# Ranked experts with places of 192, 128 and 64 rows, the outer two with transposed gate and up products

## The chip, the cores and the metric

One NeuronCore of a Trainium2 chip. The metric is the device time of one execution in microseconds (us). Engines: PE is TensorE's matmul side and PEld its loads of stationary operands, DVE is VectorE, ACT ScalarE, POOL GpSimd, SP SyncE, which issues most DMAs.

## What is computed

Two layers of a backbone on 256 context and 512 latent tokens of width 1024. Each layer mixes tokens and then runs a mixture of 16 experts, of which every token takes two. Layer 0 routes all 768 tokens (1536 pairs of token and expert), layer 1 the 512 latent ones (1024 pairs). The part that the change touches is this:

```python
def moe_ffn(h, w_router, b_router, w_e_gate, w_e_up, w_e_down):
    ...
    hid = jax.nn.silu(rows @ w_e_gate[e]) * (rows @ w_e_up[e])
    return hid @ w_e_down[e]
    ...
    return jnp.einsum("nk,nkd->nd", weight.astype(h.dtype), pair_out)
```

`rows` are the tokens of one expert. Gate and up are 1024 x 512, down is 512 x 1024, all float32. How many rows an expert has depends on the router and is known only while the kernel runs.

## The kernel before

`backbone` runs for each layer the mixers, `merge` (which ends with the router's logits), `route` and `moe`. The experts' stage is `moe`.

**Products in three parts.** A float32 operand is split into a high part (ScalarE rounds it to float32r) and a low part (VectorE subtracts, L2228), and a product is high x high + high x low + low x high, three matmuls each (`mm3`, L1323 to L1330). The first operand of a matmul is the stationary one, which TensorE loads (PEld), the second is streamed past it.

**Which expert runs where.** `route` counts the rows of the experts. Experts 15 and 14 run first, in that order. The others get ranks: those with over 128 rows first, then the rest by number (L2116 to L2126). The first `R.nd` ranks (4 in layer 0, 2 in layer 1) have places for two blocks of 128 rows, the other ranks one block. `ORDER` (L39) says in which order the ranks run. The expert of a rank is read from `R.exps` into a register of SyncE when its weights are to be loaded (L2303). What has no place is run behind the rest by `chain` (L2326), one block of 128 rows per pass, each with all six units of weights.

**One expert** (`run`, L2290). Six weight units of 1 MB each (two halves of gate, of up and of down) are loaded by SyncE's queue and split (`unit`, L2214). `front` (L2231) gathers a block of 128 rows by an indirect DMA of POOL, transposes it with eight matmuls against the identity (L2251) and splits it into `xh` and `xl`, 128 x 8 x 128 each. `front` of the next expert is issued ahead of this expert's `gate_up`. `gate_up` (L2257) has the rows as stationary operand and 512 columns of weights as the streamed one: 24 matmuls into one PSUM bank for gate, 24 for up. The activation makes the hidden rows, 128 x 512. `down` (L2273) transposes them with four matmuls (L2279), splits them (L2280, L2281), runs 2 x 12 matmuls of 512 columns, scales on ScalarE (L2286) and scatters with an indirect DMA of POOL (L2287).

PSUM has eight banks: one for the transposes of x, four for gate and up, one for the transposes of the hidden rows, two for down. `HILO` (5 and 6) is the number of buffers of split weight units. In layer 0 the tables of layer 1's S5 branch (`s5_build`) are worked out between the experts.

The order of instructions on each engine is set by the tile framework's scheduler from the program's order and its own estimate of times.

Of the kernel before, what the change touches and what calls it, by code (L numbers as in the profile page):

```python
# [7 lines left out]
F32 = mybir.dt.float32  # L8
F32R = mybir.dt.float32r
# [8 lines left out]
NT = 6  # L18

# [19 lines left out]
ORDER = ((4, 0, 5, 6, 1, 7, 8, 2, 9, 10, 3, 11, 12, 13), (2, 3, 4, 5, 0, 6, 7, 8, 1, 9, 10, 11, 12, 13))  # L39


def const_blob():
# [16 lines left out]
        tok=p[:, None] + 128 * np.arange(6)[None, :], exp=np.arange(16)[None, :] * 768 + 0 * k,  # L59
# [1926 lines left out]
def route(K, l, lg, R):  # L1986
# [12 lines left out]
    n = NT - T0  # L1999
# [116 lines left out]
    over = tl([128, 14], "over")  # L2116
    inc, pre_, a0 = (tl([128, 14], x) for x in ("inc", "pre_", "a0"))
    V.tensor_scalar(over, cnt[:, 0:14], 128.5, None, op0=OP.is_gt)
    V.tensor_tensor_scan(inc, K.c("one")[:, 0:14], over, 0.0, OP.mult, OP.add)
    V.tensor_sub(pre_, inc, over)  # L2120
    V.scalar_tensor_tensor(a0, num[:, 0:14], inc[:, 13:14], pre_, op0=OP.add, op1=OP.subtract)
    V.tensor_sub(pre_, pre_, a0)
    V.tensor_mul(pre_, pre_, over)
    ranks = tl([128, 15], "ranks")
    V.tensor_add(ranks[:, 0:14], a0, pre_)
    V.tensor_copy(ranks[:, 14:15], num[:, 14:15])  # L2126
    er = tl([1, 14, 14], "er")
    V.tensor_tensor(er, ranks[0:1, None, 0:14].to_broadcast([1, 14, 14]), num[0:1, 0:14, None].to_broadcast([1, 14, 14]), op=OP.is_equal)
# [6 lines left out]
    V.scalar_tensor_tensor(tm.rearrange("p k t e -> p (k t) e"), ranks[:, None].to_broadcast([128, 2 * n, 15]), 1.0,  # L2135
                           sel[:, :, :, 0:15].rearrange("p k t e -> p (k t) e"), op0=OP.add, op1=OP.mult)
# [22 lines left out]
    V.tensor_scalar(c, cnt[0:1], 127.0, None, op0=OP.add)  # L2159
# [3 lines left out]
    V.tensor_scalar(c, c, -1.0, 0.0, op0=OP.add, op1=OP.max)  # L2163
    dbl = tl([1, 16], "dbl")
    V.memset(dbl, 0.0)
    V.scalar_tensor_tensor(dbl[:, 0:14], ranks[0:1, 0:14], float(R.nd), over[0:1], op0=OP.is_lt, op1=OP.mult)
    V.tensor_sub(c, c, dbl)
# [10 lines left out]
    V.tensor_add(a_, a_, dbl[:, None, :].to_broadcast(shp))  # L2178
    V.scalar_tensor_tensor(a_, a_, 1.0, b_, op0=OP.add, op1=OP.mult)
    V.tensor_mul(b_, b_, num[0:1, None, :].to_broadcast(shp))  # L2180
    V.tensor_reduce(o_[:, 1:13], b_, axis=AX.X, op=OP.add)
    V.scalar_tensor_tensor(a_, b_, 6.0, a_, op0=OP.mult, op1=OP.add)
# [8 lines left out]
def moe(K, l, fd, metad, R, pd, ra, na, routing, rest, tds):  # L2191
# [39 lines left out]
    def front(c, src):  # L2231

        if c:
            tok, pair, wt = (a[:, src:src + 1] for a in (c.tok, c.pair, c.wt))
        else:
            mt = p.tile([128, 4], I32, tag="mt", bufs=4, name="mt")
            nc.sync.dma_start(mt, src)
            wt = p.tile([128, 1], F32, tag="wt", bufs=4, name="wt")
            nc.vector.tensor_scalar(wt, mt[:, 2:3].bitcast(F32), 0.5, None, op0=OP.mult)
            tok, pair = mt[:, 0:1], mt[:, 1:2]  # L2240
        x = p.tile([128, D], F32, tag="x", bufs=2, name="x")
        nc.gpsimd.memset(x, 0.0)
        gathers.append(nc.gpsimd.indirect_dma_start(out=x[:], out_offset=None, in_=fd,
                                                    in_offset=bass.IndirectOffsetOnAxis(ap=tok, axis=0),
                                                    bounds_check=ntok - 1, oob_is_err=False))
        xh = p.tile([128, 8, 128], F32R, tag="xh", bufs=3, name="xh")
        xl = p.tile([128, 8, 128], F32R, tag="xl", bufs=3, name="xl")
        for g in range(2):
            ps = pp.tile([128, 512], F32, tag="t", bufs=1, name="pt")
            for k in range(4):  # L2250
                nc.tensor.transpose(ps[:, k * 128:(k + 1) * 128], x[:, (4 * g + k) * 128:(4 * g + k + 1) * 128], K.c("id"))  # L2251
            h_, l_ = (a[:, 4 * g:4 * g + 4].rearrange(f) for a in (xh, xl))
            nc.scalar.activation(h_, ps, AF.Copy)
            nc.vector.tensor_sub(l_, ps, h_.bitcast(F32))
        return pair, wt, xh, xl

    def gate_up(frs, us):  # L2257
        gu = [[], []]
        for j in range(2):
            for i, (_, _, xh, xl) in enumerate(frs):  # L2260
                ps = pp.tile([128, 512], F32, tag="g", bufs=4, name="pg")
                mm3(nc, ps, [(xh[:, k], xl[:, k], us[2 * j + k // 4][0][:, k % 4], us[2 * j + k // 4][1][:, k % 4]) for k in range(8)])
                gu[i].append(ps)
        hds = []
        for i in range(len(frs)):
            hd = p.tile([128, 512], F32, tag="hd", bufs=2, name="hd")
            nc.scalar.activation(hd, gu[i][0], AF.Tanh, scale=0.5)
            nc.vector.scalar_tensor_tensor(hd, hd, 1.0, gu[i][0], op0=OP.add, op1=OP.mult)
            nc.vector.tensor_mul(hd, hd, gu[i][1])
            hds.append(hd)  # L2270
        return hds

    def down(fr, hd, us):  # L2273
        pair, wt, _, _ = fr
        hh = p.tile([128, 4, 128], F32R, tag="hh", bufs=2, name="hh")
        hl = p.tile([128, 4, 128], F32R, tag="hl", bufs=2, name="hl")
        ps = pp.tile([128, 512], F32, tag="h", bufs=1, name="ph")
        for k in range(4):
            nc.tensor.transpose(ps[:, k * 128:(k + 1) * 128], hd[:, k * 128:(k + 1) * 128], K.c("id"))  # L2279
        nc.scalar.activation(hh.rearrange(f), ps, AF.Copy)  # L2280
        nc.vector.tensor_sub(hl.rearrange(f), ps, hh.rearrange(f).bitcast(F32))  # L2281
        o = p.tile([128, D], F32, tag="o", bufs=2, name="o")
        for n in range(2):
            ps = pp.tile([128, 512], F32, tag="d", bufs=2, name="pd")
            mm3(nc, ps, [(hh[:, k], hl[:, k], us[n][0][:, k], us[n][1][:, k]) for k in range(4)])
            nc.scalar.activation(o[:, 512 * n:512 * n + 512], ps, AF.Copy, scale=wt)  # L2286
        nc.gpsimd.indirect_dma_start(out=pd, out_offset=bass.IndirectOffsetOnAxis(ap=pair, axis=0),  # L2287
                                     in_=o[:], in_offset=None, bounds_check=2 * ntok - 1, oob_is_err=False)

    def run(work, first=False):  # L2290


        kw = dict(alone=not first)
        frs = [front(*x) for x in work[0][1]]
# [6 lines left out]
        for i, (e, ranked, _) in enumerate([(w[0], len(w) > 2, 0) for w in work]):  # L2301
# [17 lines left out]
    blocks = metad.rearrange("(b p) c -> b p c", p=128)  # L2319
    order = ORDER[l]  # L2320
    run([(15, [(R.first, 0)]), (14, [(R.ranked, 14)])]
        + [(r, [(R.ranked, r)] + ([(R.ranked, 15 + r)] if r < R.nd else []), True) for r in order], True)
# [3 lines left out]
    def chain(j):  # L2326

        with tc.If(n > j):
            if j == 0:
                for k in range(2):  # L2330
                    for t in range(R.row.shape[2]):
                        nc.gpsimd.indirect_dma_start(out=metad, out_offset=bass.IndirectOffsetOnAxis(ap=R.row[:, k, t:t + 1], axis=0),
                                                     in_=R.ent[:, k, t], in_offset=None, bounds_check=16 * T - 1, oob_is_err=False)
            e = nc.values_load(R.over[0:1, 1 + j:2 + j], min_val=0, max_val=15)
            b = nc.values_load(R.over[0:1, 13 + j:14 + j], min_val=0, max_val=95)
            run([(e, [(None, blocks[bass.ds(b, 1)].rearrange("a p c -> p (a c)"))])])
# [47 lines left out]
def backbone(nc, tc, I, out, off):  # L2384
# [37 lines left out]
    for l in range(2):  # L2422
# [21 lines left out]
        R.nd = 4 if l == 0 else 2  # L2444
# [59 lines left out]
```

## Time and profile before

| | |
|---|---|
| median of 3 runs | 2721.1 us (2712.81 to 2722.15) |
| the profiled execution | 2708.16 us |
| its span, first to last instruction | 2706.4 us |
| PE busy | 2381.9 us (88%), 17551 matmuls |
| PEld busy | 1919.3 us (71%), 17551 loads |
| DVE busy | 1894.2 us (70%) |
| ACT busy | 1228.0 us (45%) |
| mean granted clock of TensorE | 0.92 of full speed |

All durations come from the profiled execution, one run of the program recorded by the hardware profiler. Busy time of the matmuls is no rate: they overlap, and their ends are modelled, so the start of one to the start of the next is what one costs. The granted clock is 1.00 at 2.4 GHz and 0.50 at 1.2 GHz.

### The profile page before, as it was taken

The numbers are of one execution on the slowest core, as the hardware profiler recorded it, in microseconds if no ns is written. First come the engines' busy times: TensorE is split into PE (matmuls) and PEld (weight loads), VectorE is DVE, ScalarE is ACT, GpSimd is POOL, SyncE is SP. The second block draws the span as 40 slices with busy tenths as digits, with TensorE's granted clock in tenths as the row PEclk, the third lists the DMA queues.
The fourth block names the chain that finished last, engine by engine and source line by source line (L and its number), as shares of the span: only waits on it lengthen the run. The fifth ranks groups of instructions, "written<-read, shape, count | busy, mean of one in ns | idle before, by whom it ended". The sixth has DMA issues, their size and how long they took to land. (4 is left out here: it accounts for less than half of the span.)

```text
span 2706.4 us, 46025 instructions
## 1 busy us (share of the span) xinstructions
PE 2381.9 (88%) x17551; PEld 1919.3 (71%) x17551; DVE 1894.2 (70%) x3917; ACT 1228.0 (45%) x1933; POOL 201.4 (7%) x220
## 2 busy tenths in 40 slices
PE   6999999999987894988989399999998877699993
PEld 4887668878865773776767288987786556588872
DVE  5857767864564957896778654677676586787785
ACT  4232233455533212655656332343666442476672
POOL 0000000000000000221221000000000000132210
PEclk8999999999986996999999699999997589799997
DMA  7488753431523764776778654443341085698884
GB/s 291 151 303 275 240 181 96 152 95 59 175 77 128 236 225 159 287 275 246 275 270 292 248 169 137 132 134 125 122 132 49 7 281 205 232 379 300 316 297 155
DMA packets 233719, 534.96 MB, mean 198 GB/s; under 512 B 86054, under 2 KB 116486, under 8 KB 207878
## 3 DMA queue, kind: packets, MB, share of 16 engines
q1 hardware_dynamic: 222534, 510.83, 55.2%
q0 software_dynamic: 10944, 20.99, 2.2%
q8 instruction: 142, 2.33, 0.3%
q14 instruction: 99, 0.81, 0.1%
HBM read 452.34 MB, written 100.35 MB: 204 GB/s over the span
## 5 line engine op out<-in xcount | busy, mean ns | idle before, releaser
L2228 DVE TENSOR_TENSOR lo<-raw,hi 128x2048 fp32r<-128x2048 f32 x192 | 437.8, 2289 | 87.7 <-ACT hi L2226 86.2
L2226 ACT ACTIVATE hi<-raw 128x2048 fp32r<-128x2048 f32 x192 | 364.6, 1914 | 100.5 <-PE pg L1330 71.8
L1328 PE MATMUL pg<-ah,wh 128*128 128x512 f32 (+1 forms) x768 | 280.2, 365 | 4.2 <-ACT gst L1748 4.0
L1330 PE MATMUL pg<-ah,wl 128*128 128x512 f32 (+1 forms) x768 | 280.0, 365 | 0.7 <-DVE wl L1319 0.7
L1329 PE MATMUL pg<-al,wh 128*128 128x512 f32 (+1 forms) x768 | 279.8, 364 | 0.0
L1329 PE MATMUL pg<-lo,xh 128*128 128x512 f32 x608 | 246.9, 407 | 12.6 <-DVE lo L2228 12.5
L1328 PE MATMUL pg<-hi,xh 128*128 128x512 f32 x608 | 243.9, 406 | 12.5 <-ACT hi L2226 11.9
L1319 DVE TENSOR_TENSOR wl<-wr,wh 128x512 fp32r<-128x512 f32 (+3 forms) x208 | 164.9, 795 | 118.9 <-ACT wh L1318 113.6
L1330 PE MATMUL pg<-hi,xl 128*128 128x512 f32 x608 | 244.1, 403 | 0.0
L1318 ACT ACTIVATE wh<-wr 128x512 fp32r<-128x512 f32 (+3 forms) x208 | 148.0, 715 | 211.4 <-PE pg L1329 83.7
L1328 PEld LDWEIGHTS pg<-ah,wh 128*128 128x128 f32 x768 | 147.5, 192 | 29.6 <-ACT gst L1748 5.0
L1330 PEld LDWEIGHTS pg<-ah,wl 128*128 128x128 f32 x768 | 147.4, 192 | 23.9 <-issue 1.9
L1329 PEld LDWEIGHTS pg<-al,wh 128*128 128x128 f32 x768 | 147.3, 192 | 22.1 <-issue 1.8
L1328 PE MATMUL pt<-wh,ah 128*128 128x256 f32 (+1 forms) x544 | 156.6, 289 | 2.1 <-ACT zst L1593 2.1
L1329 PE MATMUL pt<-wl,ah 128*128 128x256 f32 (+1 forms) x544 | 156.9, 289 | 0.0
L1330 PE MATMUL pt<-wh,al 128*128 128x256 f32 (+1 forms) x544 | 156.7, 288 | 0.0
L1329 PEld LDWEIGHTS pg<-lo,xh 128*128 128x128 f32 x608 | 117.6, 193 | 42.7 <-DVE lo L2228 19.0
L1328 PEld LDWEIGHTS pg<-hi,xh 128*128 128x128 f32 x608 | 116.9, 193 | 39.2 <-ACT hi L2226 14.7
L1330 PEld LDWEIGHTS pg<-hi,xl 128*128 128x128 f32 x608 | 117.1, 193 | 22.7
L1328 PE MATMUL pd<-hi,hh 128*128 128x512 f32 x304 | 120.1, 395 | 4.9 <-ACT hh L2280 4.9
L1328 PE MATMUL pc<-ah,wh 128*128 128x512 f32 (+3 forms) x352 | 120.4, 343 | 0.8 <-ACT ust L1556 0.7
L1329 PE MATMUL pc<-al,wh 128*128 128x256 f32 (+3 forms) x352 | 120.6, 343 | 0.0
(727 smaller groups left out, 5340.9 us busy)
## 6 DMA issues: line engine op xcount, KB each, us to landing
raw<-in_w_e_gate SPq DMA_DIRECT2D x64, 1024.0 KB
raw<-in_w_e_up SPq DMA_DIRECT2D x64, 1024.0 KB
raw<-in_w_e_down SPq DMA_DIRECT2D x64, 1024.0 KB
w<-in_wm SPq DMA_DIRECT2D x80, 512.0 KB
wr<-in_w_gate SPq DMA_DIRECT2D x128, 256.0 KB
wr<-in_win SPq DMA_DIRECT2D x40, 512.0 KB
gd<-gst SPq DMA_DIRECT2D x32, 384.0 KB
g<-gd SPq DMA_DIRECT2D x32, 384.0 KB
```

What stands on the lines that cost most here:

```text
L1318: nc.scalar.activation(h, r, AF.Copy)
L1319: nc.vector.tensor_sub(l, r, h.bitcast(F32))
L1328: nc.tensor.matmul(out, ah, bh, start=(i == 0), stop=False)
L1329: nc.tensor.matmul(out, ah, bl, start=False, stop=False)
L1330: nc.tensor.matmul(out, al, bh, start=False, stop=(i == n - 1))
L2226: nc.scalar.activation(h, r, AF.Copy)
L2228: nc.vector.tensor_sub(l_, r, h.bitcast(F32))
```

## The change

Ranks are by row count, largest first (a comparison of every expert's count with every other). The first `TRI` ranks (4 and 2) have places of 192 rows, those up to `WIDE` (11 and 5) of 128, the rest (3 in layer 0, 9 in layer 1) of 64. Experts 15 and 14 keep 128. The extra passes start behind these places, in blocks of 128 rows.

`front` takes the number of rows. At 192 it gathers 128 and 64 rows and puts their transposes beside each other. At 64 the high and the low part of x lie beside each other in one tile.

At 192 and 64 rows gate and up use the new `columns`: the stationary operand is a 128 x 128 piece of the weights, and x is streamed past it, 192 columns, or 128 (high and low part at once) and 64. The result is already transposed, so `down` needs no transposes of the hidden rows there. At 64 rows the two halves of the result are added on the way out of PSUM. At 128 rows the products are as before. `hd`, `hh` and `hl` have one buffer in place of two, `xh` and `xl` two in place of three.

```diff
+STRIDE = 896
+TRI = (4, 2)
+WIDE = (11, 5)
...
-ORDER = ((4, 0, 5, 6, 1, 7, 8, 2, 9, 10, 3, 11, 12, 13), (2, 3, 4, 5, 0, 6, 7, 8, 1, 9, 10, 11, 12, 13))
+ORDER = ((4, 0, 11, 5, 1, 6, 7, 2, 12, 8, 3, 9, 10, 13), (2, 5, 0, 6, 7, 3, 8, 9, 1, 10, 11, 4, 12, 13))
...
+    key = tl([128, 14], "key")
+    V.scalar_tensor_tensor(key, cnt[:, 0:14], 16.0, num[:, 0:14], op0=OP.mult, op1=OP.subtract)
+    gt = tl([128, 14, 14], "gt")
+    V.tensor_tensor(gt, key[:, None, :].to_broadcast([128, 14, 14]), key[:, :, None].to_broadcast([128, 14, 14]), op=OP.is_ge)
     ranks = tl([128, 15], "ranks")
...
+    V.tensor_reduce(ranks[:, 0:14], gt, axis=AX.X, op=OP.add)
...
+    def front(m, srcs):
+        xs, blocks = [], []
+        for nm in ("xh", "xl")[0:1 if m == 64 else 2]:
+            xs.append(p.tile([128, 1536], F32R, tag=nm, bufs=2, name=nm))
+        if m == 64:
+            xx = xs[0][:, 0:1024].rearrange("p (k s n) -> p k s n", k=8, s=2)
+            parts = [xx[:, :, 0], xx[:, :, 1]]
         else:
...
+            parts = [t[:, 0:8 * m].rearrange("p (k n) -> p k n", k=8) for t in xs]
+        for b, (c, src) in enumerate(srcs):
+            r = min(m - 128 * b, 128)
...
+    def columns(fr, us, j):
+        m, xs, _ = fr
+        nb_ = 1 if m == 64 else 2
+        w = 128 if m == 64 else 192
+        ps = [pp.tile([128, 512], F32, tag="g", bufs=4, name="pg") for _ in range(nb_)]
+        for k in range(8):
+            hi, lo = (x[:, k % 4] for x in us[2 * j + k // 4])
+            for q in range(4):
+                b, i = divmod(q, 4 // nb_)
+                c = slice(128 * q, 128 * q + 128)
+                o = ps[b][:, w * i:w * i + w]
+                first, last = k == 0 and i == 0, k == 7
+                if m == 64:
+                    nc.tensor.matmul(o, hi[:, c], xs[:, k].rearrange("p s n -> p (s n)"), start=first, stop=False, skip_group_check=True)
+                    nc.tensor.matmul(o[:, 0:64], lo[:, c], xs[:, k, 0], start=False, stop=last, skip_group_check=True)
+                else:
+                    nc.tensor.matmul(o, hi[:, c], xs[0][:, k], start=first, stop=False, skip_group_check=True)
+                    nc.tensor.matmul(o, hi[:, c], xs[1][:, k], start=False, stop=False, skip_group_check=True)
+                    nc.tensor.matmul(o, lo[:, c], xs[0][:, k], start=False, stop=last, skip_group_check=True)
+        return ps
...
+    def new(nm, m, dt=F32):
+        return p.tile([128, 768], dt, tag=nm, bufs=1, name=nm)[:, 0:4 * m]
...
+        g = []
+        for j in range(2):
+            ps = columns(fr, us, j)[0].rearrange("p (q s n) -> p q s n", q=4, s=2)
+            a = p.tile([128, 256], F32, tag="ge", bufs=2, name="ge")
+            av = a.rearrange("p (q n) -> p q n", q=4)
+            nc.scalar.activation(av, ps[:, :, 1], AF.Copy)
+            nc.vector.tensor_add(av, av, ps[:, :, 0])
+            if j == 0:
+                nc.scalar.activation(hd, a, AF.Tanh, scale=0.5)
+                nc.vector.scalar_tensor_tensor(hd, hd, 1.0, a, op0=OP.add, op1=OP.mult)
+            else:
+                nc.vector.tensor_mul(hd, hd, a)
...
+    run([(15, 128, [(R.first, 0)]), (14, 128, [(R.ranked, 14)])]
+        + [(r, 192, [(R.ranked, r), (R.ranked, 15 + r)], True) if r < R.nd else
+           (r, 128 if r < R.nw else 64, [(R.ranked, r)], True) for r in order], True)
```

## Rows read from the trace of the kernel before

**Rows 1.** Windows: stretch, length; busy us (instructions) per engine; clock, DMA share, GB/s.
```profile
1080.00:1508.00 428.00, 386.87 (x1856) 307.90 (x1854) 334.26 (x508) 247.37 (x257) 91.83 (x64) 0.96 0.75 267
2327.00:2665.00 338.00, 328.80 (x1554) 269.05 (x1550) 264.65 (x199) 227.64 (x198) 71.17 (x50) 0.98 0.80 297
...
2480.00:2560.00 80.00, 80.00 (x382) 66.46 (x381) 61.82 (x44) 55.69 (x50) 19.00 (x15) 1.00 0.84 302
```
**Rows 2.** Groups by form, whole span: busy us, mean ns, idle before and releaser.
```profile
L1328 PE MATMUL pg<-hi,xh 128*128 128x512 f32 x608 | 243.9, 406 | 12.5 <-ACT hi L2226 11.9 <-ACT xh L2253 0.7
L1328 PE MATMUL pd<-hi,hh 128*128 128x512 f32 x304 | 120.1, 395 | 4.9 <-ACT hh L2280 4.9
L1329 PEld LDWEIGHTS pg<-lo,xh 128*128 128x128 f32 x608 | 117.6, 193 | 42.7 <-DVE lo L2228 19.0
L1328 PEld LDWEIGHTS pg<-hi,xh 128*128 128x128 f32 x608 | 116.9, 193 | 39.2 <-ACT hi L2226 14.7 <-ACT xh L2253 1.1 <-issue 0.2
```
**Rows 3.** Timeline of PE in layer 1's experts: start us, length, instruction (seven between).
```profile
2433.47 0.60 PE L2251 MATMUL pt<-cb,x 128*128 128x128 f32 x4
...
2453.64 0.39 PE L1330 MATMUL pg<-hi,xl 128*128 128x512 f32 x1
...
2455.46 0.39 PE L1330 MATMUL pg<-hi,xl 128*128 128x512 f32 x1
```
**Rows 4.** Timeline of PE in a stretch of matmuls of 256 columns.
```profile
154.01 0.28 PE L1330 MATMUL pt<-wh,al 128*128 128x256 f32 x1
...
154.13 0.28 PE L1328 MATMUL pt<-wh,ah 128*128 128x256 f32 x1
```
**Rows 5.** Loads by source line: duration ns min/median/max, starts, forms.
```profile
L768 PEld LDWEIGHTS gl_s<-V,kt x192: 106/110/110, 422.6 to 1831.4; 128*32 128x32 f32 x192
...
L1328 PEld LDWEIGHTS pc<-ah,wh x352: 106/188/330, 47.3 to 1695.2; 128*128 128x128 f32 x160, 128*32 128x32 f32 x16
...
L810 PEld LDWEIGHTS gl_o<-V,A x80: 186/192/192, 436.8 to 1864.6; 128*128 128x128 f32 x80
```
**Rows 6.** Timeline of PEld: eight loads for matmuls of 12 columns.
```profile
172.62 0.97 PEld L312 LDWEIGHTS dn_g<-gg,cb 128*128 128x128 f32 x8 [0.88 <-DVE gg L302]
```
**Rows 7.** Windows in layer 0's experts, columns as in rows 1.
```profile
1304.00:1308.00 4.00, 2.22 (x11) 1.61 (x10) 4.00 (x4) 3.19 (x4) 1.65 (x2) 1.00 0.96 378
1308.00:1312.00 4.00, 3.27 (x17) 2.27 (x17) 4.00 (x6) 1.45 (x4) 0.00 (x0) 1.00 0.93 340
1471.00:1475.00 4.00, 1.68 (x5) 0.86 (x5) 4.00 (x3) 1.78 (x2) 0.00 (x0) 0.99 0.96 307
1475.00:1478.00 3.00, 2.75 (x7) 2.20 (x8) 0.79 (x2) 0.00 (x0) 0.00 (x0) 0.50 0.98 317
```
**Rows 8.** PE's groups by form from 1304 to 1308, then from 1471 to 1475 us.
```profile
L1328 PE MATMUL pg<-hi,xh 128*128 128x512 f32 x3 | 1.3, 427 | 1.8 <-ACT hi L2226 1.8
...
L1108 PE MATMUL s_w<-cb,area 128*128 128x128 f32 x2 | 0.4, 270 | 0.0
...
L1328 PE MATMUL pd<-hi,hh 128*128 128x512 f32 x2 | 0.9, 446 | 0.0
...
L1328 PE MATMUL pg<-hi,xh 128*128 128x512 f32 x1 | 0.5, 494 | 1.6 <-ACT hi L2226 1.6
```
**Rows 9.** Timelines at clock 0.50: eleven loads; then PE from 1475 us (three between).
```profile
1056.70 2.42 PEld L2042 LDWEIGHTS ent<-v,hot 128*128 128x128 f32 x11 [1.71 <-DVE hot L2036]
...
1475.25 0.80 PE L1329 MATMUL pg<-lo,xh 128*128 128x512 f32 x1 [1.22 <-DVE lo L2228]
1475.84 0.63 PE L1330 MATMUL pg<-hi,xl 128*128 128x512 f32 x1
...
1477.55 0.63 PE L1328 MATMUL pg<-hi,xh 128*128 128x512 f32 x1
...
1478.38 0.39 PE L1330 MATMUL pg<-hi,xl 128*128 128x512 f32 x1
```
**Rows 10.** DMA queues from 1154 to 1168 us: packets, MB, share of 16 engines.
```profile
q0 software_dynamic: 288, 0.59, 10.9%
```

More of the change, by code (lines that the diff above doesn't have):

```diff
@@ L2158, in route @@
     ci = tl([1, 16], "ci", I32)
-    V.tensor_scalar(c, cnt[0:1], 127.0, None, op0=OP.add)
+    cap = tl([1, 16], "cap")
+    V.memset(cap, 2.0)
+    V.tensor_scalar(cap[:, 0:14], ranks[0:1, 0:14], R.nw + 0.5, 1.0, op0=OP.is_lt, op1=OP.add)
+    V.scalar_tensor_tensor(cap[:, 0:14], ranks[0:1, 0:14], R.nd + 0.5, cap[:, 0:14], op0=OP.is_lt, op1=OP.add)
+    V.scalar_tensor_tensor(c, cap, -64.0, cnt[0:1], op0=OP.mult, op1=OP.add)
+    V.tensor_scalar(c, c, 127.0, None, op0=OP.add)
     V.tensor_copy(ci, c)
@@ L2162, in route @@
     V.tensor_copy(c, ci)
[L2163 to L2167, printed above, removed]
+    V.tensor_scalar(c, c, 0.0, None, op0=OP.max)
     end = tl([1, 16], "end")
@@ L2229, in unit @@
         return hi, lo
-    def front(c, src):
-        if c:
-            tok, pair, wt = (a[:, src:src + 1] for a in (c.tok, c.pair, c.wt))
-        else:
[L2236 to L2249, printed above, removed]
-            for k in range(4):
[L2251 to L2271, printed above, removed]
@@ new lines, in new, with gate_up @@
+    def new(nm, m, dt=F32):
+        return p.tile([128, 768], dt, tag=nm, bufs=1, name=nm)[:, 0:4 * m]
+    def gate_up(fr, us):
+        m, xs, _ = fr
+        hd = new("hd", m)
+        if m == 128:
+            gu = []
+            for j in range(2):
+                ps = pp.tile([128, 512], F32, tag="g", bufs=4, name="pg")
+                mm3(nc, ps, [(xs[0][:, k], xs[1][:, k], us[2 * j + k // 4][0][:, k % 4], us[2 * j + k // 4][1][:, k % 4]) for k in range(8)])
+                gu.append(ps)
+            nc.scalar.activation(hd, gu[0], AF.Tanh, scale=0.5)
+            nc.vector.scalar_tensor_tensor(hd, hd, 1.0, gu[0], op0=OP.add, op1=OP.mult)
+            nc.vector.tensor_mul(hd, hd, gu[1])
+            return hd
+        if m == 192:
+            cs = slice(0, 384), slice(384, 768)
+            ps = columns(fr, us, 0)
+            for b in range(2):
+                nc.scalar.activation(hd[:, cs[b]], ps[b][:, 0:384], AF.Tanh, scale=0.5)
+                nc.vector.scalar_tensor_tensor(hd[:, cs[b]], hd[:, cs[b]], 1.0, ps[b][:, 0:384], op0=OP.add, op1=OP.mult)
+            ps = columns(fr, us, 1)
+            for b in range(2):
+                nc.vector.tensor_mul(hd[:, cs[b]], hd[:, cs[b]], ps[b][:, 0:384])
+            return hd
+        g = []
+        for j in range(2):
+            ps = columns(fr, us, j)[0].rearrange("p (q s n) -> p q s n", q=4, s=2)
[6 more added lines that the diff above has]
+                nc.vector.scalar_tensor_tensor(hd, hd, 1.0, a, op0=OP.add, op1=OP.mult)
+            else:
+                nc.vector.tensor_mul(hd, hd, a)
+        return hd
@@ new lines, in down @@
+    def down(fr, hd, us):
+        m, _, bl = fr
+        hh, hl = new("hh", m, F32R), new("hl", m, F32R)
+        if m == 128:
+            ps = pp.tile([128, 512], F32, tag="h", bufs=1, name="ph")
+            for k in range(4):
+                nc.tensor.transpose(ps[:, k * 128:(k + 1) * 128], hd[:, k * 128:(k + 1) * 128], K.c("id"))
+        else:
+            ps = hd
+        nc.scalar.activation(hh, ps, AF.Copy)
+        nc.vector.tensor_sub(hl, ps, hh.bitcast(F32))
+        hh, hl = (a.rearrange("p (k n) -> p k n", k=4) for a in (hh, hl))
+        for pair, wt, c, r in bl:
+            c = slice(c, c + r)
+            o = p.tile([128, D], F32, tag="o", bufs=2, name="o")[0:r]
+            for n in range(2):
+                ps = pp.tile([128, 512], F32, tag="d", bufs=2, name="pd")[0:r]
+                mm3(nc, ps, [(hh[:, k, c], hl[:, k, c], us[n][0][:, k], us[n][1][:, k]) for k in range(4)])
+                nc.scalar.activation(o[:, 512 * n:512 * n + 512], ps, AF.Copy, scale=wt)
+            nc.gpsimd.indirect_dma_start(out=pd, out_offset=bass.IndirectOffsetOnAxis(ap=pair, axis=0),
+                                         in_=o, in_offset=None, bounds_check=2 * ntok - 1, oob_is_err=False)
@@ L2290, in run @@
     def run(work, first=False):
         kw = dict(alone=not first)
-        frs = [front(*x) for x in work[0][1]]
+        fr = front(*work[0][1:3])
         if first:
@@ L2300, in run @@
                 tables = s5_build(K, 1, rb[1], lambda nm: pp.tile([128, 512], F32, tag="h", bufs=1, name=nm), tds, 2, 1)
-        for i, (e, ranked, _) in enumerate([(w[0], len(w) > 2, 0) for w in work]):
+        for i, (e, ranked) in enumerate([(w[0], len(w) > 3) for w in work]):
             if ranked:
@@ L2304, in run @@
             us = [unit(e, j, after=gathers[0] if first and i == 0 and j in AFTER else None, **kw) for j in range(4)]
-            nxt = [front(*x) for x in work[i + 1][1]] if i + 1 < len(work) else None
-            hds = gate_up(frs, us)
+            nxt = front(*work[i + 1][1:3]) if i + 1 < len(work) else None
+            hd = gate_up(fr, us)
             us = [unit(e, j, after=gathers[0] if first and i == 0 and j in AFTER else None, **kw) for j in range(4, 6)]
-            for fr, hd in zip(frs, hds):
-                down(fr, hd, us)
-            frs = nxt
+            down(fr, hd, us)
+            fr = nxt
             if first and tds:
@@ L2317, in run @@
             rb.pop().close()
-    blocks = metad.rearrange("(b p) c -> b p c", p=128)
+    blocks = metad.rearrange("(b p) c -> b p c", p=64)
     order = ORDER[l]
-    run([(15, [(R.first, 0)]), (14, [(R.ranked, 14)])]
-        + [(r, [(R.ranked, r)] + ([(R.ranked, 15 + r)] if r < R.nd else []), True) for r in order], True)
+    run([(15, 128, [(R.first, 0)]), (14, 128, [(R.ranked, 14)])]
+        + [(r, 192, [(R.ranked, r), (R.ranked, 15 + r)], True) if r < R.nd else
+           (r, 128 if r < R.nw else 64, [(R.ranked, r)], True) for r in order], True)
     rest()
```

76 lines of the change are left out of this document (37 added, 39 removed).

## The prediction, made before the changed kernel was run

> **What bounds the kernel now.** I read the windows first, then the groups by form, then the timeline of a few stretches, then the windows again for the clock. The two expert stages are 428 us and 338 us long [rows 1]. TensorE is busy in 387 and 329 of these, and in all 80 of a stretch in the middle of layer 1's stage, with VectorE at 62 and ScalarE at 56 there. Layer 1's stage is TensorE's; layer 0's has 41 us of idle TensorE in it, because the S5 tables are built beside the experts. Whatever the change does to TensorE's queue in layer 1 therefore goes into the end time one for one.
>
> What fills that queue: 608 matmuls per line for gate and up, thus 608 / 16 = 38 blocks of 128 rows, and 304 per line for down [rows 2]. All have 512 moving columns, and they follow each other at (2455.46 − 2453.64) / 8 = 0.2275 us [rows 3], so that gate and up of a block cost 48 × 0.2275 = 10.9 us and down 24 × 0.2275 = 5.5 us. Four transposes take 0.60 us with the last one's own 0.27 in it, or 0.11 each [rows 3]. One expert of one block is then 10.9 + 5.5 + 8 × 0.11 (x) + 4 × 0.11 (hidden rows) = 17.7 us.
>
> **What the reader should look at: the weight loads.** Each matmul has a load of its own, also where two neighbours have the same stationary operand: lines 1328 and 1329 both have 608 loads of x's high part [rows 2]. So nothing "rests" across instructions; after the change, too, each matmul brings its load. Under 512 columns the load is hidden. How fast can it be? At 256 columns the pitch is 0.12 us [rows 4]. With a few columns only, eight loads of 128 columns take 0.97 us, the last one's 0.19 in it: (0.97 − 0.19) / 7 = 0.111 us [rows 6]. That row is plain float32; loads of both types last 0.106 us at 32 columns and 0.186 to 0.188 at 128 [rows 5], so I take the pace to be the same for the split (float32r) operands. No row has a float32r product with fewer than 256 moving columns. Its price lies between streaming alone, 0.2275 / 512 = 0.44 ns a column, and the 0.12 us of the 256-column row; I take 0.112 us, the load's pace, since it is the row whose limit is the load.
>
> **Part by part.**
> *192 rows* (4 experts in layer 0, 2 in layer 1). Before: two blocks, 96 matmuls, 21.8 us. After: 2 × 8 × 4 × 3 = 192 matmuls of 192 columns. Streaming would be 0.085 us each, the load 0.112, so 192 × 0.112 = 21.5 us (16.4 by streaming, 23.0 at 0.12). Gone are 8 transposes of the hidden rows (−0.9), and x's second block has transposes of half the size (−0.4). Down stays at 48 matmuls of 512. −1.6 us each, −10 together.
> *64 rows* (3 in layer 0, 9 in layer 1). Before: 48 matmuls, 10.9 us. After: 64 pairs, one of 128 columns (both halves of x beside each other) and one of 64. A pair streams 192 columns, 0.085 us, but needs two loads: 128 × 0.112 = 14.3 us, +3.4 (between −5.4 and +4.5). Transposes −0.4 and −0.4. Down stays at 24 matmuls of 512 columns. +2.6 us each with the clock as it is, +31 together.
> *128 rows*: the same instructions. *Loads of weights* (DMA, and the split on ScalarE and VectorE): 96 units a layer as before. *Gathers, scatters, memsets* on POOL's queue: as many as before, those of 64 rows smaller. *Ranking*: a few small VectorE operations swapped ahead of the first ranked expert; ±1 us a layer, taken as 0. *One buffer instead of two* for the hidden rows and their halves, *two instead of three* for x: the next writer comes a whole gate and up (over 10 us) after the last reader, which covers them; without that cover each would cost up to the 5.5 us of down. *The new evacuation at 64 rows* (copy, add, product, split before down's first matmul) replaces product, transposes, split; 0 to +1 us an expert, taken as 0.
>
> **The clock.** This is the largest term. Between its loads the 64-row gate and up streams 192 columns in 0.224 us, 860 a microsecond, for 14 us on end. In layer 0's stage the granted clock stayed at 1.00 after 1304 to 1308 us, in which the engine had eleven matmuls, two of them transposes and nine of 512 columns, some 1200 columns a microsecond; after 1471 to 1475 us, with five of 512, or 640 a microsecond, it was 0.50 [rows 7, 8]. The new gate and up lies between, nearer to the stretch after which it fell, and lasts long enough; I take it that the clock falls to the lower level (1.2 GHz). There loads follow each other at (2.42 − 0.33) / 10 = 0.209 us and matmuls of 512 columns at (1477.55 − 1475.84) / 4 = 0.43 [rows 9]. Columns are then rarer still, so nothing in that phase brings the clock back; down does. In rows 9 dense work started at 1475.25 and 0.39 us matmuls are back at 1478.4. I take 5 us of gate and up at full clock (estimate; thin from about 1471, low from 1475), the other 83 loads at +0.097, +8.1 us, and 8 of down's matmuls at +0.2, +1.6. Together +9.7 on top of +2.6: 12.3 us for a 64-row expert.
>
> **The sum.** 12 × 12.3 − 10 = +138 us. Of the 41 us that TensorE idles in layer 0, waits for ScalarE and VectorE, a slower TensorE takes some away; −8. +130 us on the profiled execution's 2708.2 us is 2838; the median of the runs shown is 2721.1, 0.5% over it, so for a median I say **2850 us**.
>
> **The rivals.**
> *The clock holds.* 860 columns a microsecond is also not far under what held. Then 12 × 2.6 − 10 = +21 (with 0.11 and hidden waits +6, with 0.12 some +43): 2727 to 2764, say 2740. For it: only few rows lie close. Chance 0.20; four tenths of that within 0.5%.
> *Loads don't bind (faster).* If a load of this type of 128 columns hides behind 64 to 192 columns, the matmuls run at 0.085 us per 192 columns: 64 rows 64 × 0.085 = 5.5 instead of 10.9, 192 rows 16.4 instead of 21.8; with the transposes 12 × −6.2 + 6 × −6.7 = −115 us. Layer 1's stage would be down to some 269 us with VectorE's 265 busy us in it [rows 1], so I give it −100, 2620 us. It decides below a pitch of about 0.09. Against it: rows 5 and 6. The Trainium skill, TensorE: Matmul & The Clock Gate, section "Back-to-back issue gap", gives about 81 ns per matmul for a stream of load and matmul pairs at 128 columns and 131 ns at 512. By that rule the 64-row gate and up would be 128 × 0.081 = 10.4 us and, on the line between its two figures, the 192-row one 192 × 0.089 = 17.1, which makes 2670 us (an estimate from that page); no float32 row here is as fast, and the 512-column row is 0.2275. Chance 0.08.
> *It does not do what it says.* A ranked expert with more rows than its place runs an extra pass behind the rest. The reference's router on its inputs gives the ranked experts of layer 0 185, 170, 168, 131 | 92 to 75 | 64, 59, 52 rows and of layer 1 171, 92 | 89, 80, 53 | 51 to 25, with bars at the bounds of the places. All fit, rank 11 of layer 0 exactly. The trace bears that count out: 0.59 MB in the stretch with the scatter of the 81-row expert and the gather of the 64-row one is 145 rows of 4 KB [rows 10]. One extra pass would cost at least its unhidden 17.7 us and six loads. Chance 0.02.
>
> **How the numbers follow.** The forecast 0.68, the clock that holds 0.20, loads hidden 0.08, extra pass 0.02, small cancelling terms 0.02. Its own range: the fall after 1 us in place of 5 adds 35 loads × 0.097 × 12 = 41 us, 2891; some 64-row experts kept at full clock by the transposes between, half of them, 2790. The range of 8 in 10 goes down to the rival that holds and up to that end: **2727 to 2895 us**. A measurement of this kernel tells about 0.5% (14 us) from no change. Faster by more: 0.08. Within: 0.08 + 0.02 = 0.10. Slower: 0.82.
>
> **What the changed profile would show.** Right: gate and up at 192 and 64 columns with starts 0.11 us apart at full clock; a 192-row expert within 1 us of its old time; in each 64-row gate and up a granted clock of 0.50 after some 5 us, loads 0.21 us apart, and down's first matmuls at 0.43; layer 1's stage some 107 us longer (9 × 12.3 − 2 × 1.6), layer 0's some 22 (3 × 12.3 − 4 × 1.6 − 8). Wrong: starts at 0.06 to 0.09 us, or a clock of 1.00 all through layer 1's stage (then the loads alone count), or more than 192 splits of weights (an extra pass).

## The result and the profile after

The changed kernel takes 2809.7 us in the median (2799.1 to 2825.4, 4 runs), the kernel before on the same chip 2719.0: a ratio of 1.034, 95% interval 1.028 to 1.040, or 91 us more. The forecast was 2850, +130, with a range of 2727 to 2895. The profiled execution is the longest of the four, 2825.4 us with a span of 2823.5. It has 18991 matmuls, 1440 more than before: 6 × 96 + 12 × 80 in gate and up, less 6 × 8 + 12 × 4 transposes. 192 splits of weights ran, as before, so there was no extra pass.

The windows of the changed kernel, for the stage of layer 0's experts, the stretch between the two and the stage of layer 1's (columns as in [rows 1]: length, then busy us of PE, PEld, DVE, ACT, POOL, then the clock):

```profile
1097.00:1514.00 417.00, 399.41 (x2402) 340.32 (x2400) 325.19 (x500) 242.37 (x253) 92.09 (x64) 0.92 0.78 274
1514.00:2342.00 828.00, 706.99 (x5853) 575.77 (x5854) 554.28 (x1324) 339.92 (x658) 18.50 (x47) 0.87 0.45 145
2342.00:2783.00 441.00, 434.93 (x2408) 377.85 (x2404) 256.51 (x204) 223.31 (x203) 79.10 (x50) 0.78 0.64 228
```

Against [rows 1], layer 1's stage is 103 us longer (forecast +107), all of it TensorE's, and its clock fell from 0.98 to 0.78. Since the clock has two levels, the time at the lower one is (1 − 0.78) × 2 × 441 = 194 us, where it was 14. Layer 0's stage is 11 us *shorter* (forecast +22), with 18 us of idle TensorE in place of 41. That is the part of the forecast that failed.

The groups of the changed kernel that answer to [rows 2], by form; the first three are gate's and up's at 64 and at 192 rows, the next two the loads under the 64-row ones, the last two loads under the 192-row ones:

```profile
L2285 PE MATMUL pg<-xh,hi 128*128 128x128 f32 x768 | 237.5, 365 | 0.0
L2286 PE MATMUL pg<-xh,lo 128*128 128x64 f32 x768 | 215.8, 293 | 0.0
...
L2288 PE MATMUL pg<-xh,hi 128*128 128x192 f32 x384 | 106.9, 284 | 4.6 <-ACT xh L2265 3.7 <-ACT hi L2227 0.9
...
L2286 PEld LDWEIGHTS pg<-xh,lo 128*128 128x128 f32 x768 | 191.9, 250 | 2.1 <-issue 0.2
L2285 PEld LDWEIGHTS pg<-xh,hi 128*128 128x128 f32 x768 | 191.7, 250 | 3.0 <-issue 0.6 <-ACT o L2352 0.2
...
L2289 PEld LDWEIGHTS pg<-xl,hi 128*128 128x128 f32 x384 | 77.1, 201 | 1.0 <-issue 0.4
L2288 PEld LDWEIGHTS pg<-xh,hi 128*128 128x128 f32 x384 | 76.1, 200 | 6.0 <-ACT xh L2265 4.5 <-ACT hi L2227 1.1
```

Every matmul has its load: 768 and 768 at 64 rows, and 384 each for lines 2288 and 2289 of the 192-row form, although these two have the same stationary operand. The mean load takes 250 ns at 64 rows: a mixture of the two clock levels, as the timeline of PE shows (start, length, instruction). It is from layer 1: first a 192-row expert, then a 64-row one, then that one's down products:

```profile
2460.40 0.27 PE L2290 MATMUL pg<-xh,lo 128*128 128x192 f32 x1
2460.51 0.28 PE L2288 MATMUL pg<-xh,hi 128*128 128x192 f32 x1
2460.62 0.27 PE L2289 MATMUL pg<-xl,hi 128*128 128x192 f32 x1
...
2468.63 0.31 PE L2285 MATMUL pg<-xh,hi 128*128 128x128 f32 x1
2468.78 0.24 PE L2286 MATMUL pg<-xh,lo 128*128 128x64 f32 x1
2468.86 0.31 PE L2285 MATMUL pg<-xh,hi 128*128 128x128 f32 x1
...
2469.49 0.46 PE L2285 MATMUL pg<-xh,hi 128*128 128x128 f32 x1
2469.74 0.36 PE L2286 MATMUL pg<-xh,lo 128*128 128x64 f32 x1
2469.91 0.45 PE L2285 MATMUL pg<-xh,hi 128*128 128x128 f32 x1
...
2481.37 0.63 PE L1333 MATMUL pd<-lo,hh 128*128 128x512 f32 x1
2481.79 1.05 PE L1334 MATMUL pd<-hi,hl 128*128 128x512 f32 x2
2482.65 0.46 PE L1332 MATMUL pd<-hi,hh 128*128 128x512 f32 x1
2482.94 0.40 PE L1333 MATMUL pd<-lo,hh 128*128 128x512 f32 x1
```

192 columns start 0.11 us apart. A 64-row pair takes 2468.86 − 2468.63 = 0.23 us, and 0.42 us from 2469.49 on. Down's matmuls are 0.42 to 0.43 apart until the clock is back. The windows of the same stretch (PE alone; the clock is the third column from the right) show the fall and the return:

```profile
2462.00:2466.00 4.00, 4.00 (x40) 1.00 0.54 158
2466.00:2470.00 4.00, 4.00 (x34) 0.89 0.54 227
2470.00:2474.00 4.00, 4.00 (x17) 0.50 0.86 294
...
2482.00:2486.00 4.00, 4.00 (x23) 0.90 0.00 0
2486.00:2490.00 4.00, 4.00 (x22) 1.00 0.33 131
```

The 64-row products begin at 2465.9; some 3 us later the clock is at 0.50, and it comes back under down. TensorE is shown as 100% busy in all of these windows: the busy share tells nothing of this.

### The profile page after: what moved, and what is told of

It is laid out like the page before. It is cut to its first block, busy times and chain, and to the rows that moved or that the text cites. A ratio compares the mean times of both kernels' runs of the same rounds, so it can differ in the third digit from the quotient of the medians.

```text
span 2823.5 us, 48914 instructions
## 1 busy us (share of the span) xinstructions
PE 2521.9 (89%) x18991; PEld 2079.0 (74%) x18991; DVE 1879.5 (67%) x3911; ACT 1217.5 (43%) x1933; POOL 209.8 (7%) x220
## 5 line engine op out<-in xcount | busy, mean ns | idle before, releaser
L2229 DVE TENSOR_TENSOR lo<-raw,hi 128x2048 fp32r<-128x2048 f32 x192 | 438.1, 2289 | 209.6 <-ACT hi L2227 202.4
L2285 PE MATMUL pg<-xh,hi 128*128 128x128 f32 x768 | 237.5, 365 | 0.0
L2286 PE MATMUL pg<-xh,lo 128*128 128x64 f32 x768 | 215.8, 293 | 0.0
L2285 PEld LDWEIGHTS pg<-xh,hi 128*128 128x128 f32 x768 | 191.7, 250 | 3.0 <-issue 0.6
L2286 PEld LDWEIGHTS pg<-xh,lo 128*128 128x128 f32 x768 | 191.9, 250 | 2.1 <-issue 0.2
L1332 PE MATMUL pd<-hi,hh 128*128 128x512 f32 (+1 forms) x304 | 134.4, 442 | 6.5 <-ACT hh L2343 6.5
L1333 PE MATMUL pd<-lo,hh 128*128 128x512 f32 (+1 forms) x304 | 131.8, 433 | 0.0
L1334 PE MATMUL pd<-hi,hl 128*128 128x512 f32 (+1 forms) x304 | 123.2, 422 | 0.0
```

The lines of the kernel that those rows point to most:

```text
L1332: nc.tensor.matmul(out, ah, bh, start=(i == 0), stop=False)
L1333: nc.tensor.matmul(out, ah, bl, start=False, stop=False)
L1334: nc.tensor.matmul(out, al, bh, start=False, stop=(i == n - 1))
L2229: nc.vector.tensor_sub(l_, r, h.bitcast(F32))
L2285: nc.tensor.matmul(o, hi[:, c], xs[:, k].rearrange("p s n -> p (s n)"), start=first, stop=False, skip_group_check=True)
L2286: nc.tensor.matmul(o[:, 0:64], lo[:, c], xs[:, k, 0], start=False, stop=last, skip_group_check=True)
```

## The experiments

All times are medians; ratios are to the kernel before on the same chip. The experiments ran on three chips, on which the kernel before took 2722.8 us (e1, e2, e4, e5), 2714.2 (e3, e8, e9, e10) and 2707.3 (e11, e12, e13), so rows are best compared by their ratios. The last three columns are the windows of one profiled execution of each kernel (us). The stretch between the stages has the same TensorE instructions in all of them but e11_before_tables and e12_no64_tables.

| kernel | time | ratio (95%) | layer 0's experts | between | layer 1's experts |
|---|---|---|---|---|---|
| before | 2721.1 | 1 | 428 | 819 | 338 |
| after | 2809.7 | 1.034 (1.028–1.040) | 417 | 828 | 441 |
| e1_no64 | 2669.7 | 0.981 (0.973–0.989) | 393 | 807 | 334 |
| e2_both | 2710.6 | 0.995 (0.991–0.998) | 404 | 827 | 358 |
| e3_plain64 | 2672.8 | 0.986 (0.983–0.989) | 398 | 813 | 336 |
| e4_packed64 | 2691.8 | 0.989 (0.987–0.992) | 398 | 830 | 338 |
| e5_plain192 | 2809.5 | 1.031 (1.024–1.039) | 426 | 830 | 423 |
| e8_no64_plain192 | 2725.0 | 1.005 (1.002–1.007) | 418 | 840 | 334 |
| e9_no64_packed192 | 2709.7 | 0.999 (0.997–1.001) | 416 | 833 | 331 |
| e10_before_halves | 2730.7 | 1.005 (1.003–1.008) | 438 | 835 | 339 |
| e11_before_tables | 2702.0 | 0.999 (0.996–1.001) | 371 | 869 | 337 |
| e12_no64_tables | 2721.2 | 1.005 (1.002–1.008) | 378 | 884 | 336 |
| e13_no64_tri41 | 2664.7 | 0.983 (0.980–0.987) | 393 | 825 | 325 |

### Which part costs: no 64-row places, and the clock held

**e1_no64**

```diff
-WIDE = (11, 5)
+WIDE = (14, 14)
```

> No 64-row places (WIDE = 14 in both layers): those experts run as 128-row blocks, all else as changed (ranking, order, single buffers, transposed 192-row products). Theory (loads at 0.112 us, and the clock, both only in the 64-row products): what is left of the change is 6 x -1.6 us, so 2700 to 2720 us, the kernel before or 0.4% under it, granted clock in layer 1's experts near 1.00. Rival (the order, the single buffers or the 192-row form make it slower): stays well over before, 2760 us or more.

Measured 2669.7, 30 us under the lowest end. With its 64-row form the kernel takes 140 us more (2809.7 − 2669.7), and what is left of the change is *faster* than the kernel before by some 50 us. By the windows, 107 us of the first difference lie in layer 1's experts and 24 in layer 0's; 21 lie between the stages, where TensorE's instructions are the same, and no run shows that the form causes these. The windows of e1_no64:

```profile
1087.00:1480.00 393.00, 373.02 (x2169) 314.35 (x2168) 326.06 (x496) 243.49 (x250) 95.20 (x64) 0.97 0.82 291
1480.00:2287.00 807.00, 690.62 (x5853) 567.36 (x5853) 552.24 (x1324) 340.40 (x658) 18.52 (x47) 0.89 0.46 149
2287.00:2621.00 334.00, 327.92 (x1724) 273.60 (x1722) 261.04 (x195) 226.12 (x194) 74.58 (x50) 0.97 0.82 301
```

Layer 1 is back at [rows 1] but for 4 us; layer 0 is 35 us under it, where the 192-row experts of both stages had been forecast to give 10 together.

**e2_both**

```diff
-                    nc.tensor.matmul(o[:, 0:64], lo[:, c], xs[:, k, 0], start=False, stop=last, skip_group_check=True)
+                    nc.tensor.matmul(o, lo[:, c], xs[:, k].rearrange("p s n -> p (s n)"), start=False, stop=last, skip_group_check=True)
```

> As changed, but the second matmul of each 64-row pair streams both halves of x, 128 columns in place of 64 (the low x low product is then in the sum, too). No load more or less. Theory: loads bind, so the pitch stays 0.112 us; 256 columns in 0.224 us, 1140 a microsecond, is near the stretch after which the clock held, so it holds: gate and up 14.3 us each, 80 us off the changed kernel (63 of half-clock loads, 18 of half-clock down), 2730 us. Rival A (the clock has no part, loads alone and waits made it slower): 2810 us as changed. Rival B (streaming binds): 12 x 64 x 64 columns x 0.44 ns = +22 us, 2830 us.

Measured 2710.6, 20 us under the expected 2730, and both rivals fall: with *more* columns streamed the kernel is 99 us faster than the change. Layer 1's window, and products of one 64-row expert in the timeline:

```profile
2314.00:2672.00 358.00, 351.30 (x2401) 302.44 (x2400) 255.23 (x203) 223.50 (x203) 75.09 (x50) 0.98 0.77 281
```

```profile
2437.79 0.28 PE L2286 MATMUL pg<-xh,lo 128*128 128x128 f32 x1
2437.90 0.28 PE L2285 MATMUL pg<-xh,hi 128*128 128x128 f32 x1
2438.01 0.27 PE L2286 MATMUL pg<-xh,lo 128*128 128x128 f32 x1
```

Starts are 0.11 us apart as before, so the load sets the pace at 64 columns and at 128 alike, and the clock is 0.98. This separates the two terms of the 64-row form in layer 1: the loads alone (358 − 334) / 9 = 2.7 us an expert, the clock (441 − 358) / 9 = 9.2 us.

**e3_plain64** (64-row places with x stationary and three products of 512 columns)

```diff
+                else:
+                    mm3(nc, t[0:64], [(pair[b](k)[:, 0], pair[b](k)[:, 1], *ws[k]) for k in range(8)])
```

> The 64-row places stay, but untransposed: x of 64 rows stationary (64 columns), three products of 512 columns as for 128 rows. If it is the transposed form alone that costs (128-column loads at a pitch of 0.112 us and the clock), the time is that of e1_no64, 2660 to 2680 us, and the clock holds in layer 1. If places of 64 rows themselves cost (gathers, transposes of 64 rows, a clock that falls for half-used rows of the array), it is above 2700 us.

Measured 2672.8, as e1_no64. So places of 64 rows by themselves cost nothing, nor do products with 64 stationary columns bring the clock down in layer 1. The window of its experts (clock 0.98):

```profile
2292.00:2628.00 336.00, 326.89 (x1716) 233.89 (x1716) 252.52 (x185) 219.47 (x184) 81.59 (x50) 0.98 0.82 300
```

**e4_packed64** (x's halves side by side as the stationary operand, 32 products of 512 columns instead of 48)

```diff
+                        nc.tensor.matmul(t, x.rearrange("p s n -> p (s n)"), ws[k][0], start=(k == 0), stop=False, skip_group_check=True)
+                        nc.tensor.matmul(t[0:64], x[:, 0], ws[k][1], start=False, stop=(k == 7), skip_group_check=True)
...
+                    nc.scalar.activation(a, ps[b, j][64:128], AF.Copy)
+                    nc.vector.tensor_add(a, a, t)
```

> 64-row experts with x as the stationary operand again, high and low part side by side as its 128 columns: weights' high half streamed past both (512 columns), low half past x's high part, 32 matmuls of 512 columns in place of 128 small ones; the two halves of the result are added over partitions on ScalarE and VectorE. Theory: 32 x 0.2275 = 7.3 us against 10.9 before and 14.3 or more as changed, dense columns, clock held: 12 x (-3.6 - 0.4) - 10 = -58 us on before, 2660 us, if VectorE (0.35 us more per expert) doesn't take the lead. Rival (64-row places themselves, their gathers or evacuations cost the time): 2780 us or more.

Measured 2691.8, a miss: slower than e1_no64 in spite of 17 us less work on TensorE in layer 1. Its window there:

```profile
2309.00:2647.00 338.00, 310.84 (x1579) 233.18 (x1576) 262.35 (x204) 228.88 (x202) 105.32 (x50) 0.93 0.80 298
```

TensorE idles 27 us instead of 6, and the clock is 0.93 instead of 0.97. Some 11 us of its waits are for the hidden rows behind the longer way out of PSUM, as many for the halves of x. Most of the difference lies outside the experts (830 against 807).

### Where layer 0's gain comes from

**e5_plain192** (the change, but 192-row experts as a block of 128 and a block of 64 rows)

```diff
+                if r == 128:
+                    mm3(nc, t, [(xs[0][:, k], xs[1][:, k], *ws[k]) for k in range(8)])
...
+                    mm3(nc, t[0:64], [(pair[b](k)[:, 0], pair[b](k)[:, 1], *ws[k]) for k in range(8)])
```

> 192-row experts as rows again, a block of 128 and one of 64, 512 columns of weights streamed, three matmuls each; 64-row experts as changed. Theory: 192 loads at 0.112 us are the same 21.5 us as 96 x 0.2275, so only the hidden rows' transposes come back: +5 to +10 us on the changed kernel, 2815 us (within 0.5%). Rival (the transposed 192-row form is a gain or a loss of its own, 5 us an expert or more): 30 us off the changed kernel, either way.

Measured 2809.5. Beside slow 64-row experts the form of the 192-row ones makes no difference to the time: layer 0 is 9 us longer than after the change, at the same clock of 0.92, and layer 1 is 18 us shorter, at 0.81 against 0.78.

**e8_no64_plain192** (the edits of e1_no64 and e5_plain192 together)

```diff
-WIDE = (11, 5)
+WIDE = (14, 14)
...
+                if r == 128:
+                    mm3(nc, t, [(xs[0][:, k], xs[1][:, k], *ws[k]) for k in range(8)])
...
+                    mm3(nc, t[0:64], [(pair[b](k)[:, 0], pair[b](k)[:, 1], *ws[k]) for k in range(8)])
```

> No 64-row places (as in e1_no64), and the 192-row experts are run untransposed too, as a block of 128 and a block of 64 rows in turn: 48 products of 512 columns for each instead of 192 of 192 columns in gate and up together for each block, 21.8 us of TensorE against 21.5. What is left of the change is the ranking by count, the narrower second block and the buffers. Theory A (the gain of some 35 us in layer 0's stage comes from the 192-row form: it goes through a weight unit once and lets it go, where two blocks in turn hold the units longer, so ScalarE and VectorE can split the next unit earlier): most of the gain is lost, layer 0's stage is back at 410 to 427 us with TensorE waiting on split units for 20 us, and the time is 2690 to 2715 us. Theory B (the gain lies in the narrower second block and the buffers): layer 0's stage stays at 393 to 402 us, and the time at 2670 to 2682 us.

Measured 2725.0, 11 us over the kernel before on that chip and 10 over theory A's range, with layer 0's stage inside A's 410 to 427 us: the stage's gain comes with the 192-row form; the narrower second block, the ranking and the buffers give at most 10 of its 35 us (428 against 418). Of the difference in time to e1_no64, 25 us lie in that stage and 33 between the stages, which this doesn't explain. Its windows beside those of e1_no64 above:

```profile
1088.00:1506.00 418.00, 382.62 (x1816) 289.28 (x1815) 329.58 (x503) 244.39 (x256) 92.33 (x64) 0.97 0.76 274
1506.00:2346.00 840.00, 712.92 (x5857) 582.84 (x5857) 554.93 (x1326) 342.20 (x658) 18.62 (x47) 0.87 0.44 143
2346.00:2680.00 334.00, 326.14 (x1540) 258.57 (x1540) 261.42 (x197) 226.12 (x198) 78.73 (x50) 0.99 0.81 301
```

Layer 0's stage has 35 us of idle TensorE (20 in e1_no64) and 10 us more work. The waits of PE in that stage (us in total, times, longest), first of e8_no64_plain192:

```profile
PE pg L1334 <- ACT hi L2229: 11.7, 6, 2.3
PE pt L2265 <- DVE xl L2274: 6.2, 5, 2.9
PE pg L1335 <- DVE lo L2231: 6.0, 8, 1.2
```

and of e1_no64:

```profile
PE pt L2262 <- DVE xl L2266: 6.7, 3, 5.5
PE pd L1332 <- ACT hh L2343: 4.3, 3, 2.8
PE pg L1333 <- DVE lo L2229: 2.6, 4, 1.0
```

The waits for split units of weights (18 us against 3) are most of what the 192-row form takes away there.

**e10_before_halves** tries the obvious reason, that the 192-row form lets a unit go earlier.

```diff
-                mm3(nc, ps, [(xh[:, k], xl[:, k], us[2 * j + k // 4][0][:, k % 4], us[2 * j + k // 4][1][:, k % 4]) for k in range(8)])
+            for h in range(2):
+                hi, lo = us[2 * j + h]
+                for i, (_, _, xh, xl) in enumerate(frs):
+                    for k in range(4 * h, 4 * h + 4):
...
```

> The kernel before, and nothing of the change: only the experts with two blocks run their gate and up with both blocks on one half of a weight matrix before the next half, so that a weight unit is let go after 24 products (5.5 us) rather than held through the other half's 24 and the second block. The same products in number and size. Theory A (release of units): TensorE's waits on split units in layer 0 (some 20 us) go, and the time falls by 15 to 30 us, to 2690 to 2705. Theory B: no change, 2710 to 2722 us.

Measured 2730.7, against both theories: slower by 0.5%, with layer 0's stage 10 us longer with 42 us of idle TensorE as against 41. TensorE's waits for split units came to 28 us in that stage (20 in the kernel before). My theory of the early release fell.

```profile
1084.00:1522.00 438.00, 396.12 (x1844) 312.30 (x1844) 334.21 (x508) 247.04 (x258) 99.32 (x64) 0.95 0.74 261
```

**e11_before_tables** and **e12_no64_tables** put the S5 tables behind the experts, the first in the kernel before, the second in e1_no64.

```diff
-S5STEP = 4
+S5STEP = 0
```

> The kernel before, with the tables of layer 1's S5 branch put behind layer 0's experts in the program's order instead of four steps behind each expert. The question is where layer 0's waits for split units come from (41 us of idle TensorE in the kernel before, 35 in e8_no64_plain192, 20 in e1_no64). Theory T: VectorE's table work, which the scheduler lays among the splits; then the stage of layer 0's experts loses most of its idle time and is 385 to 400 us here, within 10 us of e12_no64_tables, and the tables cost their own time behind it (some 40 to 70 us). Theory F: the products of two 128-row blocks themselves hold the units too long; then the stage stays at 415 us or more.

> e1_no64 with the tables put behind layer 0's experts in the same way. Theory T: the stage of layer 0's experts is 375 to 390 us, within 10 us of e11_before_tables' (TensorE's own work differs by 10). Theory F: 20 us or more below e11_before_tables' stage, as e1_no64 is below e8_no64_plain192.

Layer 0's stage and the stretch behind it, of e11_before_tables:

```profile
1078.00:1449.00 371.00, 360.93 (x1754) 295.80 (x1751) 305.42 (x423) 236.31 (x209) 85.12 (x56) 1.00 0.81 292
1449.00:2318.00 869.00, 711.38 (x5954) 581.01 (x5952) 580.89 (x1414) 352.97 (x706) 20.20 (x55) 0.87 0.45 145
```

and of e12_no64_tables:

```profile
1081.00:1459.00 378.00, 361.21 (x2072) 305.12 (x2072) 299.22 (x410) 232.15 (x200) 86.96 (x56) 0.97 0.79 287
1459.00:2343.00 884.00, 730.38 (x5954) 594.43 (x5952) 583.85 (x1410) 353.33 (x706) 20.20 (x55) 0.84 0.44 143
```

Theory T holds, with e11_before_tables' stage 14 us under the range that it gave. Without the tables beside them the experts of the kernel before run 371 us, and those with the 192-row form 378: the form by itself gives nothing that shows, though the clock was 1.00 in the one and 0.97 in the other. The tables lengthen the stage by 428 − 371 = 57 us in the kernel before and by 393 − 378 = 15 us in e1_no64. Of the 57, TensorE's idle time is 31 (41 against 10) and its busy time 26, at a clock of 0.96 against 1.00; of the 15, the idle time is 3 (20 against 17) and the busy time 12, at 0.97 in both. So the gain of 35 us appears only where the tables' work lies beside the experts. That it is the order in which the scheduler lays that work is the likely reading, but no run held the order fixed, so it is not shown. Put behind, the tables cost 50 us (869 − 819) and 77 us (884 − 807) there, in a stretch that varies by 33 us by itself, so neither kernel is better for it. Why the kernel with the 192-row form hides the tables better stays open; letting units go earlier did not do it in e10_before_halves.

### A better version

**e9_no64_packed192** (e8_no64_plain192 with the packed product of e4_packed64 for the second block, which `PACK` picks; the edit is shown against e8_no64_plain192)

```diff
-PACK = {192: False}
+PACK = {192: True}
```

> No 64-row places; the 192-row experts as blocks of 128 and 64 rows, the second with its high and low halves side by side as one stationary of 128 columns: 32 products of 512 columns in its gate and up instead of 48, and one copy and one sum more on ScalarE and VectorE for each of gate and up. If TensorE's instructions set these stages: 6 experts by 16 products of 0.2275 us is 22 us less than e8_no64_plain192. If the longer chain of evacuations is what counts (as e4_packed64 hints), no better than e8_no64_plain192, or worse by 6 experts by some 2 us.

Measured 2709.7, 15 us under e8_no64_plain192, between the two expectations: TensorE has 10 us less work in layer 0's stage and 5 in layer 1's, but it idles 43 us in layer 0's, and the stages are only 2 and 3 us shorter. It loses to e1_no64.

**e13_no64_tri41**

```diff
-TRI = (4, 2)
-WIDE = (11, 5)
+TRI = (4, 1)
+WIDE = (14, 14)
```

> e1_no64 with one place of 192 rows instead of two in layer 1, where only one ranked expert has over 128 rows. Gone from TensorE's queue in that stage: 192 products of 192 columns become 48 of 512 (21.5 to 10.9 us), 24 of down's 48 products (5.5 us) and one block's transposes. If the stage is TensorE's, it falls by some 16 us to 317 us, and the time to some 2653 us; if the splits on VectorE (261 us busy) set it, by less than 8. Layer 0's stage and the stretch between the stages have the same instructions as e1_no64: they say how far 393 and 808 us come again.

```profile
1080.00:1473.00 393.00, 373.16 (x2168) 315.02 (x2167) 325.81 (x495) 243.49 (x249) 95.12 (x64) 0.96 0.81 291
1473.00:2298.00 825.00, 702.89 (x5856) 576.13 (x5857) 554.29 (x1326) 341.30 (x658) 18.57 (x47) 0.87 0.45 146
2298.00:2623.00 325.00, 310.83 (x1544) 254.34 (x1544) 257.99 (x190) 223.22 (x189) 70.03 (x47) 0.98 0.83 310
```

Measured 2664.7, over the expected 2653. Layer 1 gave 9 us of the 16 expected: TensorE's work fell by 17 and its idle time rose from 6 to 14 us, in waits for ScalarE's and VectorE's results. Against e1_no64 the ratios to the kernel before overlap (0.980 to 0.987, 0.973 to 0.989), so the two are not told apart; both beat the kernel before by 1.7 to 1.9%. Layer 0's stage came out at 393 again, the stretch between at 825 instead of 807 with the same instructions.

## Why the prediction was right, and where it was not

**The pace of the loads: right.** Starts were to be 0.11 us apart at 192 and at 64 columns; they are, and 128 columns at the same pace in e2_both show that it is the load. This settles the rival that the loads hide. The Trainium skill's page TensorE: Matmul & The Clock Gate, section "Back-to-back issue gap", has 81 ns for such a pair at 128 columns; the trace doesn't agree for these operands, at 0.11 us.

**64 rows at full clock: right.** +2.6 us an expert forecast, 2.7 measured in layer 1 (e2_both against e1_no64).

**The clock: right in layer 1, too large in layer 0.** +9.7 us an expert forecast, 9.2 measured in layer 1. The lower level lasted (194 − 14) / 9 = 20 us an expert, where the prediction's terms make 83 × 0.209 + 8 × 0.43 = 20.8; the 14 us are e2_both's, (1 − 0.98) × 2 × 358. The split was off: of 1476 steps from load to load in the 64-row products of both layers (those under 0.4 us) 606 are longer than 0.18 us, 50 an expert instead of 83; the rest of the slow time fell on down and on the 128-row neighbours. In layer 0 the slow time was (1 − 0.92) × 2 × 417 = 67 us against (1 − 0.96) × 2 × 404 = 32 in e2_both, 12 us an expert, give or take 3 for the two digits of the clock. There the 64-row form costs (417 − 393) / 3 = 8 us an expert in all, not 12.3. The rival in which the clock holds has its case in e2_both: 2710.6 us at a clock of 0.98 in layer 1, where that rival named 2740.

**192 rows: near for the form, wrong for the kernel.** "−1.6 us each" counted TensorE's instructions, which makes 6 us less for the four of layer 0. Without the tables the two forms' stages have the same 361 us of TensorE work, the 192-row one at the lower clock (0.97 against 1.00). But with the tables the stage gains 35 us.

**The step that failed** is the end of the sum: "Of the 41 us that TensorE idles in layer 0 ... a slower TensorE takes some away; −8". It took the idle time as a given of the kernel and let only the slow 64-row experts fill it. The runs show in its place that this idle time, and with it what the tables cost beside the experts, changes with the form of the other experts: 41 us of idle TensorE and 57 us for the tables in the kernel before, 20 and 15 in e1_no64. Layer 0 was to be +22 and was −11, by 3 × 8 − 35. That the order of ScalarE's and VectorE's work is behind it is argued, not shown.

**That the total came close is luck in part.** The two profiled executions are 117 us apart (2825.4 − 2708.2), where the sum said +130. Layer 0's stage is 33 us under its forecast and layer 1's 4, but 25 us that nobody forecast lie outside the stages: 9 between them and 16 in the rest of the span, with the same products in both kernels. The changed ranking is not what lengthens these: e3_plain64, which has it too, begins layer 0's stage at 1081 us and has 813 between the stages, where the changed kernel has 1097 and 828 and the kernel before 1080 and 819. So an error of 33 us was mostly made up by stretches that differ from kernel to kernel anyway. The medians are 91 us apart and not 117, since the profiled execution of the changed kernel lies 16 us over its median and that of the kernel before 11 under.

Two small slips change nothing: the +6 of the lower end comes out nearer +7, and the upper end is 2850 + 41 = 2891, not 2895.

## What to carry to other kernels

Before turning a product round so that the weights are stationary, divide the streamed columns by the measured pace of a load: a column takes 0.2275 / 512 us here [rows 3] and a load 0.112, so that under some 250 columns of these split operands the load sets the pace; fewer columns per load save nothing and may cost the clock, while e2_both got 99 us back by streaming columns that were not needed. Where a scheduler orders the engines, treat idle time of the bound engine beside foreign work as something that an edit can move (here a stage by 10 us one way in e10_before_halves and 35 the other in e1_no64), and try each part of a change alone: here one part cost 131 us in the two stages and hid 39 that the rest had won there.

## What was not expected of the hardware

- With the same loads at the same pace of 0.11 us the granted clock went both ways: with 128 and 64 columns in turn it was 0.50 some 3 us after 2465.9, with 128 and 128 it was 0.98 over layer 1's whole stage, with 192 it was 1.00 up to 2466.
- Products with 64 stationary columns in place of 128 (e3_plain64) did not bring it down: 0.98 in layer 1's stage.
- The stretch between the experts' stages, with the same TensorE instructions, took 807 to 840 us in eleven kernels, with clocks of 0.89 to 0.86: (1 − 0.89) × 2 × 807 = 178 us at the lower level in the shortest, (1 − 0.87) × 2 × 840 = 218 in the longest. The two lengths differ by 33 us and the slow times by 40; since a load or a matmul of 512 columns at the lower level takes about twice its time (0.21 against 0.112 us, 0.43 against 0.2275), the clock accounts for some 20 of the 33 (an estimate). What decides how much of it is slow, and what the rest is, was not tried.
